# A copy-and-scale kernel that is limited by DMA: loads and stores moved into one queue in a fixed order

## The chip, the cores and the metric

The kernel runs on one core of one Trainium2 chip. The metric is the device time of one execution in microseconds (us), the median of several runs. A profile of one execution goes with it; its span is the time from the first to the last instruction on the core.

## The reference: what is computed

```python
def setup_inputs():
    batch, seq, hidden, n_experts = 16, 1024, 512, 8
    k = 2
    # x: [batch, seq, hidden] float32, expert_weights: [batch, seq, k] float32

def reference(x, expert_indices, expert_weights):
    x_expanded = x[:, :, np.newaxis, :].repeat(k, axis=2)
    weights = expert_weights[..., np.newaxis]
    return (x_expanded * weights).astype(np.float32)
```

Each of the 16,384 tokens has a row of 512 float32 numbers. The output holds two copies of each row, each multiplied by one weight. The indices are not used. So 33.55 MB of x go in and 67.11 MB go out, and there is one multiplication for each output element.

## The kernel before

Tokens are laid out with 128 consecutive ones in each partition (`A_TOTAL` = 128). One row of x in a partition has 2 KB, one row of the output (`row` = 1024 elements) 4 KB. The kernel takes 8 tiles of 16 tokens per partition. A tile of x is 32 KB in each partition, 4.19 MB in all; it is read in one transfer. The output is made in halves of 8 tokens, also 32 KB per partition, and each half is stored in one transfer.

```python
    xr = x.rearrange("b s h -> (b s) h").rearrange("(p a) h -> p (a h)", a=A_TOTAL)
    outr = out.rearrange("b s k h -> (b s) (k h)").rearrange(
        "(p a) n -> p (a n)", a=A_TOTAL)
    # ... (wr: the weights in the same layout)
    TX = 16
    TO = 8
    x_pool = ctx.enter_context(tc.tile_pool(name="x_pool", bufs=2))
    o_pool = ctx.enter_context(tc.tile_pool(name="o_pool", bufs=4))

    w_tile = w_pool.tile([P, A_TOTAL * k], f32)
    nc.sync.dma_start(out=w_tile, in_=wr)

    for i in range(A_TOTAL // TX):                      # 8 tiles
        x_tile = x_pool.tile([P, TX * hidden], f32)
        nc.scalar.dma_start(                            # loads: queue of ScalarE
            out=x_tile, in_=xr[:, i * TX * hidden : (i + 1) * TX * hidden])
        for j in range(TX // TO):                       # 2 halves
            o_tile = o_pool.tile([P, TO * row], f32)
            for t in range(TO):
                # ...
                for kk in range(k):
                    nc.vector.tensor_scalar(            # one row of 512, times one weight
                        out=o_tile[:, o : o + hidden],
                        in0=x_tile[:, at : at + hidden],
                        scalar1=w_tile[:, c : c + 1],
                        scalar2=None, op0=mybir.AluOpType.mult)
            first = (i * TX + j * TO) * row
            nc.sync.dma_start(                          # stores: queue of SyncE
                out=outr[:, first : first + TO * row], in_=o_tile)
```

Loads and stores are in two queues. A load can start as soon as one of the two x buffers is free, whatever the stores are doing. VectorE must wait when all four output buffers are still being stored.

Of the kernel before, what the change touches and what calls it, by code (L numbers as in the profile page):

```python
# [1 line left out]

# [4 lines left out]


@with_exitstack
def kernel(  # L10
    ctx: ExitStack,
    tc: tile.TileContext,
    x: bass.AP,
    expert_indices: bass.AP,
    expert_weights: bass.AP,
    out: bass.AP,
):
    nc = tc.nc

    batch, seq, hidden = x.shape  # L20
    k = expert_weights.shape[-1]
    P = nc.NUM_PARTITIONS
    ntok = batch * seq
    assert ntok % P == 0
    A_TOTAL = ntok // P

    xr = x.rearrange("b s h -> (b s) h").rearrange("(p a) h -> p (a h)", a=A_TOTAL)
    outr = out.rearrange("b s k h -> (b s) (k h)").rearrange(
        "(p a) n -> p (a n)", a=A_TOTAL
    )  # L30
    wr = expert_weights.rearrange("b s k -> (b s) k").rearrange(
        "(p a) k -> p (a k)", a=A_TOTAL
    )
    f32 = mybir.dt.float32
    row = k * hidden

    TX = 16
    TO = 8

    w_pool = ctx.enter_context(tc.tile_pool(name="w_pool", bufs=1))  # L40
    x_pool = ctx.enter_context(tc.tile_pool(name="x_pool", bufs=2))
    o_pool = ctx.enter_context(tc.tile_pool(name="o_pool", bufs=4))

    w_tile = w_pool.tile([P, A_TOTAL * k], f32)
    nc.sync.dma_start(out=w_tile, in_=wr)

    for i in range(A_TOTAL // TX):
        x_tile = x_pool.tile([P, TX * hidden], f32)
        nc.scalar.dma_start(
            out=x_tile, in_=xr[:, i * TX * hidden : (i + 1) * TX * hidden]  # L50
        )
        for j in range(TX // TO):
            o_tile = o_pool.tile([P, TO * row], f32)
            for t in range(TO):
                at = (j * TO + t) * hidden
                for kk in range(k):
                    c = (i * TX + j * TO + t) * k + kk
                    o = t * row + kk * hidden
                    nc.vector.tensor_scalar(  # L59
                        out=o_tile[:, o : o + hidden],  # L60
                        in0=x_tile[:, at : at + hidden],
                        scalar1=w_tile[:, c : c + 1],
                        scalar2=None,
                        op0=mybir.AluOpType.mult,
                    )
            first = (i * TX + j * TO) * row
            nc.sync.dma_start(out=outr[:, first : first + TO * row], in_=o_tile)


# [1 line left out]
_INS = ['x', 'expert_indices', 'expert_weights']  # L71
_OUTS = [((16, 1024, 2, 512), 'float32')]


# [23 lines left out]
```

## Time and profile before

| what | value |
|---|---|
| time, median of 3 runs | 241.06 us (240.87 to 241.54) |
| span of the profiled execution | 238.8 us |
| bytes moved by DMA | 100.81 MB: 33.69 MB read from HBM, 67.11 MB written |
| mean rate over the span | 422 GB/s |
| stores: 16 of 4.19 MB | median 44.9 us from issue to landing |
| loads of x: 8 of 4.19 MB | median 23.9 us from issue to landing |
| load of the weights: 1 of 0.13 MB | 10.1 us from issue to landing |
| one `tensor_scalar`, 128 x 512 float32 | 480 ns long; they overlap, 16 of them take 6.42 us |

The time from issue to landing includes the time in which a transfer stands behind others in its queue, or takes turns with those of the other queue. Queue q1 in the profile is that of SyncE (the weights and the stores), q10 that of ScalarE (the loads of x). A queue's share is the time that its packets took, as a share of the time of all 16 DMA engines over the span. A row of digits cuts the span into 40 slices, each digit giving the busy share in tenths. The DMA's packets have the size of one row in one partition: 32 KB for loads and stores, 1 KB for the weights, and 4 bytes for a completion signal.

### The profile page before, as it was taken

To read this page: it belongs to the slowest core of one execution; us is meant where nothing else is said; L and a number is where in the kernel's file an instruction comes from. 1 tells how busy PE (TensorE), PEld (TensorE's weight loads), DVE (VectorE), ACT (ScalarE), POOL (GpSimd) and SP (SyncE) were. 2 spreads that over 40 slices of the span, in tenths; PEclk is the share of its full clock that TensorE was granted. 3 is DMA by queue.
4 is the path that set the end of the run, shared out by engine and by line. 5 is a ranking of instruction groups with operands and counts; after the bars stand their busy time and mean duration, and the time that the engine had idled before them with its cause. 6 is when DMAs were issued, how large, how long until landed. Compare 5 with 4: busy or idle time off the path is not lost.

```text
span 238.8 us, 358 instructions
## 1 busy us (share of the span) xinstructions
DVE 102.5 (43%) x256; POOL 0.2 (0%) x4
## 2 busy tenths in 40 slices
DVE  0079994059701904682054910739008486400000
POOL 0000000000000000000000000000000000000000
DMA  7999999999999999999999999999999999999994
GB/s 277 447 439 417 434 380 417 439 439 439 423 423 428 439 423 412 439 439 439 439 439 434 434 439 439 412 435 428 428 423 434 434 439 439 439 439 434 434 439 214
DMA packets 3602, 100.81 MB, mean 422 GB/s; under 512 B 400, under 2 KB 528, under 8 KB 528
## 3 DMA queue, kind: packets, MB, share of 16 engines
q1 hardware_dynamic: 2448, 67.24, 65.4%
q10 hardware_dynamic: 1152, 33.55, 33.2%
q14 instruction: 2, 0.02, 0.0%
HBM read 33.69 MB, written 67.11 MB: 422 GB/s over the span
## 4 chain that ended last, share of the span: by engine, by line
DMA 62%; DVE 18%; another core or an unknown queue 5%; DVEq 0%; issue 0%
DMA out_dram<-o_tile 57%; DVE o_tile L59 18%; DMA x_tile<-in_x_dram 5%; DVEq L93 0%; DVEq L59 0%
## 5 line engine op out<-in xcount | busy, mean ns | idle before, releaser
L59 DVE TENSOR_SCALAR o_tile<-x_tile,w_tile 128x512 f32<-128x512 f32 x256 | 102.5, 480 | 103.3 <-DMA out_dram<-o_tile 74.1
L82 POOL MEMSET const-bfloat16-1.0<- 128x1 bf16 x1 | 0.1, 101 | 0.0
L82 POOL MEMSET const-uint8-127<- 128x1 uint8 x1 | 0.1, 101 | 0.0
L82 POOL MEMSET const-float32-0.0<- 128x1 f32 x1 | 0.1, 98 | 0.2 <-issue 0.2
L82 POOL MEMSET const-float32-1.0<- 128x1 f32 x1 | 0.1, 98 | 0.0
## 6 DMA issues: line engine op xcount, KB each, us to landing
out_dram<-o_tile SPq DMA_DIRECT2D x16, 4096.0 KB, 44.9
x_tile<-in_x_dram ACTq DMA_DIRECT2D x8, 4096.0 KB, 23.9
w_tile<-in_expert_weights_dram SPq DMA_DIRECT2D x1, 128.0 KB, 10.1
```

The lines of the kernel that those rows point to most:

```text
L59: nc.vector.tensor_scalar(out=o_tile[:, o : o + hidden], in0=x_tile[:, at : at + hidden], scalar1=w_tile[:, c : c + 1], scalar2=None, op0= ...
L82: nc = _bacc.Bacc("TRN2", target_bir_lowering=False, num_devices=1)
```

## The change

Loads and stores are all issued by SyncE into one queue, in an order that the program fixes. Of a pool of three slots of 64 KB per partition, each slot takes one tile: x is loaded into its upper half, VectorE writes the two scaled copies over the whole slot, and the slot is stored in one transfer of 64 KB per partition. The order of the tokens makes that safe: the outputs of token t take the place of x rows that have been used, and the last row is scaled in place. Loads stay at 32 KB per partition, but stores double in size, and there are 8 in place of 16. The weights move to the queue of ScalarE. The aim is that reads and writes of HBM come in long stretches in a fixed order and do not take turns packet by packet, and that fewer and larger transfers are made.

```diff
-    TX = 16
-    TO = 8
+    T = 16
+    SLOTS = 3
+    n_tiles = A_TOTAL // T
 ...
-    x_pool = ctx.enter_context(tc.tile_pool(name="x_pool", bufs=2))
-    o_pool = ctx.enter_context(tc.tile_pool(name="o_pool", bufs=4))
+    pool = ctx.enter_context(tc.tile_pool(name="slots", bufs=SLOTS))
 ...
-    nc.sync.dma_start(out=w_tile, in_=wr)
+    nc.scalar.dma_start(out=w_tile, in_=wr)
 ...                      (the loop of the kernel before is taken out)
+    x_at = T * (row - hidden)
+    slots = {}
+
+    def load(i):
+        slots[i] = pool.tile([P, T * row], f32, name="slot")
+        nc.sync.dma_start(
+            out=slots[i][:, x_at : x_at + T * hidden],
+            in_=xr[:, i * T * hidden : (i + 1) * T * hidden],
+        )
+
+    def scale(i):
+        slot = slots[i]
+        for t in range(T):
+            src = slot[:, x_at + t * hidden : x_at + (t + 1) * hidden]
+            for kk in range(k):
+                o = t * row + kk * hidden
+                c = (i * T + t) * k + kk
+                nc.vector.tensor_scalar(
+                    out=slot[:, o : o + hidden],
+                    in0=src,
+                    scalar1=w_tile[:, c : c + 1],
+                    scalar2=None,
+                    op0=mybir.AluOpType.mult,
+                )
+
+    def store(i):
+        nc.sync.dma_start(
+            out=outr[:, i * T * row : (i + 1) * T * row], in_=slots.pop(i)
+        )
+
+    for i in range(SLOTS):
+        load(i)
+    scale(0)
+    store(0)
+    for i in range(1, n_tiles):
+        scale(i)
+        store(i)
+        if i - 1 + SLOTS < n_tiles:
+            load(i - 1 + SLOTS)
```

In SyncE's queue this gives: load 0, load 1, load 2, store 0, store 1, load 3, store 2, load 4, store 3, load 5, store 4, load 6, store 5, load 7, store 6, store 7. Load 3 uses the slot of tile 0 and has to wait until store 0 has landed; load 4 waits for store 1, and so on.

More of the change, by code (lines that the diff above doesn't have):

```diff
@@ L35 @@
     row = k * hidden
-    TX = 16
-    TO = 8
+    T = 16
+    SLOTS = 3
+    n_tiles = A_TOTAL // T
     w_pool = ctx.enter_context(tc.tile_pool(name="w_pool", bufs=1))
-    x_pool = ctx.enter_context(tc.tile_pool(name="x_pool", bufs=2))
-    o_pool = ctx.enter_context(tc.tile_pool(name="o_pool", bufs=4))
+    pool = ctx.enter_context(tc.tile_pool(name="slots", bufs=SLOTS))
     w_tile = w_pool.tile([P, A_TOTAL * k], f32)
-    nc.sync.dma_start(out=w_tile, in_=wr)
[L47 to L50, printed above, removed]
-        )
[L52 to L67, printed above, removed]
```

## The prediction

> **What bounds the kernel now.** I read the page first: the busy time of the engines, the two DMA rows of the slices, the queue shares and the chain that ended last. Then I cut the span into stretches, and last looked at the single DMA packets.
>
> ```profile
> DVE 102.5 (43%) x256; POOL 0.2 (0%) x4
> DMA  7999999999999999999999999999999999999994
> q1 hardware_dynamic: 2448, 67.24, 65.4%
> q10 hardware_dynamic: 1152, 33.55, 33.2%
> DMA 62%; DVE 18%; another core or an unknown queue 5%; DVEq 0%; issue 0%
> L59 DVE TENSOR_SCALAR o_tile<-x_tile,w_tile 128x512 f32<-128x512 f32 x256 | 102.5, 480 | 103.3 <-DMA out_dram<-o_tile 74.1
> ```
>
> VectorE is busy 43% and spends as long waiting, mostly for a store to free an output buffer. That wait costs nothing by itself, because the DMA row stands at 9 in every slice but the first and the last: the stores are not late, they are queueing. The two data queues took 65.4 + 33.2 = 98.6% of the 16 engines' span. So only 1.4% of 238.8 us, 3.3 us, is idle DMA time. The chain's "DMA 62%" is not the measure here; a chain passes through VectorE while other transfers are running. The stretches show where the idle time and the slower spots lie (window, length, VectorE, GpSimd, clock, DMA share, GB/s):
>
> ```profile
> 0.00:20.00 20.00, 6.69 (x17) 0.20 (x4) 1.00 0.94 395
> 20.00:40.00 20.00, 18.74 (x48) 0.00 (x0) 1.00 1.00 405
> 40.00:57.00 17.00, 6.27 (x16) 0.00 (x0) 1.00 1.00 432
> 57.00:100.00 43.00, 19.43 (x49) 0.00 (x0) 1.00 1.00 433
> 100.00:180.00 80.00, 32.32 (x81) 0.00 (x0) 1.00 1.00 432
> 182.00:200.00 18.00, 11.30 (x29) 0.00 (x0) 1.00 1.00 430
> 200.00:236.00 36.00, 5.77 (x15) 0.00 (x0) 1.00 0.99 429
> ```
>
> From 40 to 180 us loads and stores share the engines, and they move 432 GB/s. After 182 us there are only stores (the last load lands at 181 us), in one queue, and they move 429 to 430. Mixed and unmixed traffic run at one speed. The packet records say the same: 2899 of the 3072 data packets (32 KB each, one per partition row) took exactly 1213 ns on their engine, loads and stores alike, so 16 x 32768 B / 1.213 us = 432 GB/s. All 3072 at that pace take 3072 x 1.213 / 16 = 232.9 us. The span is 238.8, so **everything this change could win lies in 5.9 us**, which divide so:
> - about 2.0 us before the first data packet and 1.1 us after the last one;
> - 0.5 us for the weights: 128 packets of 1 KB at 65 ns, over 16 engines; and 0.2 us for 400 semaphore packets of 9 ns;
> - 1.7 us of data packets longer than 1213 ns, nearly all of them loads. They come in bursts: the first packets of the first load (0.28 us per engine), the loads in flight when the first stores set in at 20.8 us (0.36 us), and again at 30 to 37 us (0.8 us). This is the 405 GB/s of the second stretch. Later load starts cost almost nothing (0.2 us for five of them).
>
> The remainder, some 0.4 us, is rounding and engines that end a little apart.
>
> **What the Trainium skill says.** "DMA: Bandwidth & Descriptors", section "Where 436 GB/s comes from", puts the ceiling at 435.2 GB/s for the 16 ports. The 432 of the trace agrees, and leaves 0.7% at most. The same page, "Issuing engines are not separate DMA queues", says that transfers issued from several engines run on the same 16 DMA engines and interleave; the trace agrees, one load and one store in flight together have the bandwidth of one. "Queues, rings and completion order" says that descriptors of one ring are consumed in order, and that an engine takes turns between the queues it has work for, packet by packet. The weights bear that out: 8 packets per engine taking turns with 8 packets of x should need 8 x 1.3 us, and the load of w lands after 10.1 us. So one queue replaces turns by a fixed order, not by more bandwidth. "SBUF — State Buffer", section on the SBUF size, gives about 208 KiB usable per partition. Three slots of 64 KB and 1 KB of weights fit, a fourth slot does not; no run shows that here.
>
> **The change part by part.**
> Bytes: unchanged, 33.55 MB of x in, 67.11 MB out. At 432 GB/s a load of 4.19 MB takes 9.7 us, a store of 8.39 MB 19.4 us. 232.9 us stay.
> Issues: 16 stores of 332 ns become 8, from the same SyncE; they were never on the path. Saved: eight times 16 semaphore packets of 9 ns, below 0.1 us.
> Packet size: if the 64 KB row of a store goes as one packet, one fixed cost in two is saved. An estimate from the page's 435.2 GB/s: 32768 B need 1204.7 ns, the trace has 1213, so 8.3 ns are fixed; 1024 x 8.3 ns / 16 = 0.5 us saved. If the row is split into 32 KB packets, nothing.
> VectorE: the same 256 instructions at 0.40 us pitch (16 in 6.42 us), so 12.8 us a tile. Scaling in place adds waits of VectorE on itself from token 8 on, when outputs are written over inputs; most wait for instructions finished long ago. I allow up to 2 us a tile, 13 to 15 us.
> Order: what must be shown is that the single ring never runs dry. Data begin at 2.0; x of tile 0 lands at 13.3 as now, so store 0 is issued at about 27, while loads 1 and 2 keep the ring busy to 32. Stores 0 and 1 fill it to 71. Load 3 waits for store 0 (landed at 52) and is issued 19 us before its turn. From there the ring reads load 3, store 2, load 4, store 3 and so on. A tile lands, and store and load of the ring (29 us) run while VectorE needs 15: a slack of some 14 us. The tightest place is the last one: load 7 lands at about 197, store 6 covers 19.4 us, and scaling (15), landing and starting a store (0.4 + 1.3) need 16.7. **Slack 2.7 us, so no gap.** VectorE then stays hidden everywhere, as now.
> Read starts: a load behind a store in the same ring may expose the latency of its first packets. The two clean cases of now are 0.28 and 0.36 us; five such loads give 0 to 1.6 us, in place of the 1.4 us that the bursts after 20 us cost today.
> Sum: 232.9 + 0.5 (w) + 0.2 + 0.3 (first load) + 0 to 1.6 - 0 to 0.5 + 3.1 (both ends) = 236.5 to 238.6 us of span. The remainder that I couldn't place (0.4) put on top, the middle is 237.9, against 238.8 now: **0.9 us less**, and 241.06 - 0.9 = 240.2 us.
>
> **The rivals.**
> 1. Order pays: reads and writes in separate phases run faster than mixed ones, and the gain is several per cent. For it speaks only the dip to 405 GB/s at 20 to 40 us, worth 20 x 27/432 = 1.3 us. Against it, 432 mixed and 430 stores alone. With all dips and the packet cost gone the span would be some 236.4, and the time about 238.7, still only 1%.
> 2. The ring turns around badly: each change between store and load (some 12) lets the engine drain. With 0.4 us each it is 5 us more, about 245. Against it, today engines change direction at nearly every packet without losing anything; but there the two directions sit in different queues, so the trace has no case of a load directly behind a store in one ring.
> 3. The ring runs dry, because a load stands behind a store that waits for VectorE. If the scaling took 18 us, not 13 to 15, only the last tile would show it, with 1 to 2 us. A later first store doesn't matter before 32 us.
> 4. One 64 KB packet is slower than two of 32 KB. Nothing in the profile shows such a packet, so I can't exclude it; 1% more on each is 1.6 us.
>
> **Range and chances.** The median time stands 2.3 us above the profiled span (241.06 and 238.8). A gain above 2% needs a time below 236.2, that is a span near 234, which is 232.9 us of packets plus 1.1 us for both ends: practically excluded. A loss above 2% needs 4.8 us, so rival 2 at its full size, or two rivals together. I take 238.7 to 242.6 as the range, more room above than below, since all that can go wrong adds.
>
> **What would show it.** In the profile after: the DMA shares of the queues again add up to 98% or more; the slices at 9 throughout; 430 to 434 GB/s in any stretch of the middle; store landings 19.4 us apart and loads 9.7 us when both queue; VectorE waiting for loads instead of stores, about 100 us busy. Slices that drop at every change of direction would show rival 2; a gap at about 216 us, before the last store, rival 3. A rate above 435 would show that my ceiling is wrong, and the prediction with it.

## The result, and the profile after

The changed kernel takes 250.64 us (250.4 to 250.87), the kernel before beside it 241.08. The ratio is **1.0388, with a 95% interval of 1.0362 to 1.0413: slower**. The prediction was 240.2 us, with a range to 242.6. It was wrong.

The page of the changed kernel, the same parts as shown of before: engines, DMA by slices, queues, and the group of scalings.

```profile
span 248.8 us, 333 instructions
DVE 103.3 (42%) x256; POOL 0.2 (0%) x4
DMA  7999999899899999999999999999989999999992
q1 hardware_dynamic: 2304, 100.66, 97.9%
q10 hardware_dynamic: 144, 0.13, 0.2%
L66 DVE TENSOR_SCALAR slot<-slot,w_tile 128x512 f32<-128x512 f32 x256 | 103.3, 479 | 119.2 <-DMA slot<-in_x_dram 105.1
```

The DMA engines are as busy as before, 98.1% of a longer span, and they move the same bytes. So nothing ran dry: the packets themselves took longer. Stretches of the changed kernel (window, length, VectorE, GpSimd, clock, DMA share, GB/s):

```profile
5.00:28.00 23.00, 14.36 (x36) 0.00 (x0) 1.00 0.99 428
64.00:72.00 8.00, 0.00 (x0) 0.00 (x0) 1.00 1.02 393
98.00:118.00 20.00, 1.51 (x4) 0.00 (x0) 1.00 1.01 383
128.00:150.00 22.00, 3.81 (x10) 0.00 (x0) 1.00 1.01 399
213.00:240.00 27.00, 9.45 (x24) 0.00 (x0) 1.00 0.99 430
```

Only loads (5 to 28 us) and only stores (213 to 240 us) run at 428 and 430 GB/s. Wherever the queue goes from a store to a load and back, as at 64 to 72, 98 to 118 and 128 to 150 us, it is 383 to 399 with the engines still busy. (A packet counts in the stretch in which it starts, so the rate of a short stretch is to be read with its share: 393 GB/s at a share of 1.02 are 385 for busy engines.) The DMA records show it packet by packet. An undisturbed 32 KB packet takes 1213 ns, an undisturbed 64 KB packet 2418 ns. The first loads behind a store, the last two loads ahead of a store and the last store packet ahead of a load take mostly 0.1 to 1.2 us more, the longest 1.4. I call the sum of what goes beyond the undisturbed time, divided by 16 engines, the **stretched time**: 10.9 us after, 1.7 before. A second sum is the idle DMA time in the last 12 us of transfers, because the engines end apart: 2.2 us after, 1.0 before. So +9.3 and +1.2, less 0.5 for half as many store packets, make 10.0 us, and that is the difference of the spans (248.8 and 238.8).

### The profile page after: what moved, and what is told of

The parts are those of the page before. It is cut to its first block, busy times and chain, and to the rows that moved or that the text cites. A ratio compares the mean times of both kernels' runs of the same rounds, so it can differ in the third digit from the quotient of the medians.

```text
span 248.8 us, 333 instructions
## 1 busy us (share of the span) xinstructions
DVE 103.3 (42%) x256; POOL 0.2 (0%) x4
## 4 chain that ended last, share of the span: by engine, by line
DMA 68%; DVE 21%; issue 0%; DVEq 0%; SPq 0%
DMA slot<-in_x_dram 34%; DMA out_dram<-slot 29%; DVE slot L66 21%; DMA w_tile<-in_expert_weights_dram 5%; DVEq L66 0%; SPq L54 0%
## 5 line engine op out<-in xcount | busy, mean ns | idle before, releaser
L66 DVE TENSOR_SCALAR slot<-slot,w_tile 128x512 f32<-128x512 f32 x256 | 103.3, 479 | 119.2 <-DMA slot<-in_x_dram 105.1
```

Of the source, the lines that this page charges most:

```text
L66: nc.vector.tensor_scalar(out=slot[:, o : o + hidden], in0=src, scalar1=w_tile[:, c : c + 1], scalar2=None, op0=mybir.AluOpType.mult,)
```

## The experiments

Each was compared with the kernel before on the same chip (its median there was 242.6 to 243.5 us), so ratios are compared. All compute the whole reference. The two sums at the right are each from one profiled execution. That of before is of an execution of 240.5 us in the first comparison, so the row of before serves as a mark, and the other rows are best compared with each other.

| run | queues | packets, load / store | ratio to before (95%) | stretched us | ends apart us |
|---|---|---|---|---|---|
| before | 2 | 32 / 32 KB | 1 | 1.7 | 1.0 |
| after | 1 | 32 / 64 | 1.0388 (1.0362 to 1.0413) | 10.9 | 2.2 |
| e1 | 2 | 32 / 64 | 1.0251 (1.0197 to 1.0305) | 6.5 | 0.1 |
| e2 | 1 | 32 / 32 | 1.0150 (1.0109 to 1.0192) | 6.1 | 2.8 |
| e3 | 1, 21 changes | 16 / 32 | 1.0260 (1.0202 to 1.0319) | 8.7 | 2.2 |
| e4 | 1, 5 changes | 16 / 32 | 1.0043 (1.0025 to 1.0061) | 4.1 | 1.1 |
| e5 | 2 | 32 / 32 | 0.9954 (0.9931 to 0.9976) | 2.7 | 1.7 |
| e6 | 2 | 32 / 64 | 1.0260 (1.0201 to 1.0319) | 3.1 | 2.0 |
| e7 | 1 | 32 / 16 | 1.0105 (1.0070 to 1.0140) | 4.1 | 3.2 |
| e8 | 1 | 16 / 16 | 1.0085 (1.0061 to 1.0110) | 3.0 | 3.5 |
| e9 | 1, engines staggered | 32 / 32 | 1.0355 (1.0318 to 1.0392) | 6.9 | 3.6 |
| e10 | 1, engines staggered | 32 / 64 | 1.0444 (1.0413 to 1.0475) | 10.7 | 2.2 |
| e11 | 2 | 16 / 32 | 1.0247 (1.0204 to 1.0290) | 2.7 | 6.4 |
| e12 | 1, engines staggered | 32 / 32 | 1.0161 (1.0107 to 1.0215) | 3.7 | 2.7 |

A "change" is a place where the queue goes from load to store or back; the changed kernel, e2, e7 and e8 have 11.

**e1: loads in a queue of their own.**

```diff
     def load(i):
-        nc.sync.dma_start(
+        nc.scalar.dma_start(
```

> The changed kernel with its loads issued by ScalarE into ScalarE's queue (behind the weights); slots, sizes and waits stay. Theory (a change of direction inside one queue costs about 1 us: the changed kernel has 11 of them and 11 us of stretched packets): with the loads in a queue of their own nothing changes direction inside a queue, 239 to 241 us, load packets mostly 1213 ns, 64 KB store packets 2418 ns. Rival A (the 64 KB packets are slower): stays at 249 to 251. Rival B (scaling in place in a shared slot, or three slots only, holds up the transfers): stays at 248 to 251.

It stayed at 1.025, so my theory fell in this form: one queue alone is not the cause. But the loss has another shape here. Two stretches of e1 and the last scaling of its timeline:

```profile
55.00:205.00 150.00, 51.76 (x128) 0.00 (x0) 1.00 1.01 423
215.00:230.00 15.00, 11.01 (x28) 0.00 (x0) 1.00 0.71 306
213.07 13.01 DVE L66 TENSOR_SCALAR slot<-slot,w_tile 128x512 f32<-128x512 f32 x32 [18.21 <-DMA slot<-in_x_dram]
```

The two queues take turns by packet, and with 64 KB against 32 KB the loads get a third of the engines. Load 7 is issued at 174.5 us and lands only after 38.4 us; the last store can't be issued before 226, and the engines stand idle for some 5 us (DMA share 0.71). The share of the engines is only part of that delay: load 7 is signed off by its first engine after 27.5 us, and by its last 11 us later, so far had the engines drifted apart. Stretched time is 6.5, of which 1.3 falls at 25 to 35 us, when stores set in behind the first loads.

**e2: stores cut into two transfers of 32 KB per partition**, still one queue and one order.

```diff
-            out=outr[:, i * T * row : (i + 1) * T * row], in_=slots.pop(i)
+ ...                       (slot = slots.pop(i), half = T * row // 2)
+        for h in range(2):
+            nc.sync.dma_start(
+                out=outr[:, (2 * i + h) * half : (2 * i + h + 1) * half],
+                in_=slot[:, h * half : (h + 1) * half],
+            )
```

> The changed kernel with each store cut into two transfers of 32 KB per partition, issued one behind the other into the same queue. Theory (change of direction): the number of changes stays at 11, so 250 to 252 us, with the stretched packets still next to the changes. Rival A (64 KB packets): 239 to 241, as all packets are 32 KB again.

Neither: 1.015, in between. Stretches of e2:

```profile
28.00:40.00 12.00, 11.93 (x31) 0.00 (x0) 1.00 1.01 394
66.00:88.00 22.00, 3.24 (x9) 0.00 (x0) 1.00 1.00 395
88.00:100.00 12.00, 9.70 (x25) 0.00 (x0) 1.00 1.01 437
100.00:118.00 18.00, 1.59 (x5) 0.00 (x0) 1.00 1.00 391
138.00:235.00 97.00, 38.82 (x96) 0.00 (x0) 1.00 1.00 430
```

The early changes (28 to 40, 66 to 88 and 100 to 118 us) run at 391 to 395 GB/s, but the last two loads and their four changes, all after 138 us, cost 0.5 us of stretched time together: 430. The landings of the 16 engines give a hint why. Each transfer is signed off by every engine: within 0.8 us up to 63 us, within 1.6 at 85, 3.0 at 116, and 3.9 to 4.2 from 146 us on. **The engines drift apart, and as they do, the changes become free.**

**e3 and e4: the number of changes.** Halved tiles, six slots; e3 keeps the order, e4 groups it.

```diff
-    T = 16
-    SLOTS = 3
+    T = 8
+    SLOTS = 6
 e4 besides: the loop is now
+    for g in range(0, n_tiles, SLOTS):
+        group = range(g, min(g + SLOTS, n_tiles))
+        for i in group: load(i)
+        for i in group: scale(i); store(i)
```

> Tiles of half the size (8 tokens, stores 32 KB, loads 16 KB per partition), six slots, the same order: after the first loads one load behind each store. The changes of direction rise from 11 to 21, the bytes stay. Theory (about 1 us for each change): 239.5 + 21 = 259 to 262 us. Rival C (a load's packets are slow in proportion to their bytes when they stand in one queue with stores): stays at 249 to 252. Rival A: 240 to 241.

> The same halved tiles and six slots in one queue, but in groups: six loads, six stores, six loads, six stores, four loads, four stores. 5 changes of direction. Theory (about 1 us for each change): 239.5 + 5 = 244 to 246 us. Rival C (by bytes): 249 to 252. Rival A: 240 to 241.

e4 came close to its number; e3 was far below it (its 21 changes cost 8.1 of the 8.7 us, not 21), and again its changes after 125 us were almost free, at a spread of the landings of 3.2 to 3.8 us. In e4, where the spread stays at 0.7 to 1.9 us, each change can be seen alone:

```profile
36.00:84.00 48.00, 12.17 (x31) 0.00 (x0) 1.00 1.01 435
84.00:96.00 12.00, 0.00 (x0) 0.00 (x0) 1.00 0.97 380
96.00:116.00 20.00, 17.86 (x45) 0.00 (x0) 1.00 1.00 430
124.00:174.00 50.00, 13.36 (x33) 0.00 (x0) 1.00 1.00 432
174.00:200.00 26.00, 13.14 (x33) 0.00 (x0) 1.00 1.00 411
```

Between changes 430 to 435, at the changes of 84 to 96 and 174 to 200 us 380 and 411. Its five changes cost 0.8, 1.0, 0.35, 0.7 and 0.5 us of stretched time. So a fixed cost per change fails, and so does a cost by bytes.

**e5: both taken away**, loads in their own queue and stores cut to 32 KB (the edits of e1 and e2).

> Loads in a queue of their own as in e1, and each store cut into two transfers of 32 KB per partition as in e2; slots and scaling in place stay. What the first four runs left: the single queue alone is not the cause (e1), the 64 KB packet is part of it (e2), and changes of direction inside one queue stretch the packets beside them (e4: nothing stretched but at its 5 changes). New theory: two things add, the packet size of the stores and the changes inside one queue. Then with both taken away 239.5 to 242 us, on a level with the kernel before, stretched time below 2.5 us. Rival (slots and waits cost by themselves): 244 or more.

0.9954: with both parts undone the slots and the scaling in place cost nothing, and this is the version that beats both kernels, if by half a per cent. Its stretched time of 2.7 us is just above the 2.5 that I had allowed. Its stretches:

```profile
20.00:40.00 20.00, 19.52 (x49) 0.00 (x0) 1.00 1.00 407
55.00:195.00 140.00, 53.40 (x132) 0.00 (x0) 1.00 1.00 430
195.00:236.00 41.00, 12.94 (x32) 0.00 (x0) 1.00 1.00 432
```

It runs as the kernel before did, with the same dip when the stores set in.

**e6: the kernel before with 64 KB output buffers.**

```diff
-    TO = 8                      # and o_pool bufs=4
+    TO = 16                     # and o_pool bufs=2
```

> The kernel before, with only its output buffers doubled to 64 KB (two of them), so that a store has 64 KB per partition; two queues, x buffers of its own. New theory: the 64 KB packets stretch loads that take turns with them, 4 to 6 us in all as in e1, so 244 to 249 us, some of it perhaps as a dry ring. Rival (64 KB is bad only in one queue with its changes): 240 to 241.

The time of 249.7 us is a little above the expected range, and not for the expected reason: its stretched time is only 3.1 us.

```profile
20.00:34.00 14.00, 14.00 (x37) 0.00 (x0) 1.00 0.67 242
34.00:230.00 196.00, 82.02 (x206) 0.00 (x0) 1.00 1.00 430
```

With two x buffers and whole tiles to be scaled before a store, more than 5 us of DMA time are idle at the start (share 0.67), where neither load 2 nor store 0 is issued before the first tile is scaled, at 26.8 us. So 64 KB in two queues costs here mainly by that wait. The 64 KB packets are shown to stretch others next to changes (after against e2) and in e1 (6.5 us, e5 2.7), not in general. Why e1 and e6 differ in this is open.

**e7 and e8: packets of 16 KB**, stores in four transfers, in e8 loads in two as well.

> The changed kernel, one queue and 11 changes, each store cut into four transfers of 16 KB per partition; loads stay at 32 KB. Theory that a change costs by the store packet beside it: 64 KB gave 10.9 us of stretched time, 32 KB 6.1, so 16 KB should give 3 to 4.5 and 243.5 to 246 us. Rival (16 engines that drift apart no longer change at once, which is why the later changes of e2 and e3 were free): no more than 1 us away from e2.

> As e7, and the loads also cut into two transfers of 16 KB per partition. Theory (packet size on both sides of a change): 2 to 3.5 us of stretched time, below e7 by about 1 us. Rival (only the store packets matter): the same as e7 plus 0.5 us for the larger number of packets.

Both ways a step down, to 4.1 and 3.0 us of stretched time, but the ratios fall by only 0.5 and 0.2 points, and their intervals overlap. The gain goes mostly into the packets themselves: two of 16 KB take 1222 ns where one of 32 KB takes 1213, which is 1.2 us in e7 and 0.6 more in e8; and the engines end 0.3 and 0.4 us further apart.

Stores of 64, 32 and 16 KB give 10.9, 6.1 and 4.1 us of stretched time. Most of the difference comes late. The first three changes (15 to 92 us) cost 3.2, 2.9 and 2.3 us, the eight later ones 7.3, 2.5 and 1.2. So while the engines are close together a change costs nearly the same beside 64 KB packets as beside 32 KB; what the large packets do is to keep the later changes dear. With them the engines also drift apart more slowly (2.3 us at 147 us, in e2 3.9).

**e9, e10, e12: the engines staggered from the start.** To test whether it matters that all engines change together, three small loads go ahead of everything, work for some engines only. What they write is overwritten later.

```diff
+ ...                       (slots[0] is made here; stores are cut as in e2)
+    for lo, hi in ((0, 8), (8, 12), (12, 14)):
+        nc.sync.dma_start(
+            out=slots[0][lo:hi, : T * hidden], in_=xr[lo:hi, : T * hidden])
     for i in range(SLOTS):
         load(i)
```

> e2 (one queue, stores cut to 32 KB packets) with three small loads put in front of everything, of 8, 4 and 2 rows of 32 KB, into a part of the first slot that is written over later. They are extra work for some of the 16 DMA engines only (up to three packets, 3.6 us, if 8 rows go to 8 engines, and so on), so that the engines reach each change of direction apart. In e2 a change cost 1.2 us and more while all engines landed within 0.8 us of each other, and nearly nothing once they had drifted 4 us apart. Theory (a change costs because all engines change together): the spread of the first landings is 3 to 4 us, the stretched time falls from 6.1 to 1.5 to 3.5 us, and the first change at 30 us costs less than 0.5. The time itself hardly moves (244 to 247), as the extra packets delay the last engine by as much. Rival (the early changes are dear for another reason, such as addresses or tile number): stretched time 5.5 to 6.5 us as in e2, and a time of 248 to 251.

The time and the stretched time are worse than expected, the main point is clear. Stretches of e9: the start, the first five changes (they lie later here, and each window is as long as that of e2 or longer), and the end:

```profile
5.00:15.00 10.00, 0.00 (x0) 0.00 (x0) 1.00 0.96 213
35.00:47.00 12.00, 11.93 (x31) 0.00 (x0) 1.00 1.01 432
73.00:95.00 22.00, 1.92 (x5) 0.00 (x0) 1.00 1.01 427
104.00:124.00 20.00, 3.87 (x10) 0.00 (x0) 1.00 1.02 441
138.00:235.00 97.00, 38.81 (x96) 0.00 (x0) 1.00 1.00 432
```

The changes that ran at 394, 395 and 391 GB/s in e2 now run at 432, 427 and 441. After the first 15 us, all 11 changes together cost 0.8 us of stretched time, in e2 5.4; the landings are 5.4 us apart. What made it slow is the start: at 5 to 15 us only 213 GB/s, with packets of 2 to 4 us, 6.1 us lost.

> The same three small loads in front of the changed kernel itself, with its 64 KB stores. Its engines drifted to 4 us apart as well, but its late changes still cost up to 0.9 us. Theory: a spread has to be large against a packet, and 3.6 us is only one and a half packets of 64 KB; so the stretched time falls little, from 10.9 to 8 to 10 us, and the time is 250 to 254. If it falls to 4 or less, the packet size counts only through the spread.

The total of 10.7 hides the same split: 6.3 us in the first 15 us, 4.4 after it, where the changed kernel had 10.4. So staggering takes away more than half of the cost with 64 KB packets too, with the landings 4.2 to 5.9 us apart, and not all.

In e12 the rows of the small loads are spread (every fourth partition: `slots[0][lo:hi:4]`, `xr[lo:hi:4]`, from partitions 0, 64 and 80).

> e9 with the rows of the three small loads spread out (every fourth partition, in different blocks) instead of neighbouring rows. In e9 nothing was stretched at the changes any more, but the first 15 us ran at half speed, 6.1 us lost, so that the time rose. If that loss came from neighbouring partitions being written by several DMA engines at once, it goes here: the first 15 us at over 400 GB/s, stretched time of the whole 1 to 2 us, and a time 1.000 to 1.008 of the kernel before (e2: 1.015). If the first loads are slow because the engines start apart, whatever the rows, it stays at 1.03 and over.

```profile
5.00:15.00 10.00, 0.00 (x0) 0.00 (x0) 1.00 0.92 347
28.00:40.00 12.00, 11.93 (x31) 0.00 (x0) 1.00 1.00 429
66.00:88.00 22.00, 0.45 (x2) 0.00 (x0) 1.00 0.99 413
100.00:118.00 18.00, 1.07 (x4) 0.00 (x0) 1.00 1.01 431
```

The expectation was met in part. The start loses 2.2 us in place of 6.1, at 347 GB/s and not over 400. The 11 changes cost 1.6 us; at 66 to 88 us, where the landings were 2.3 to 2.7 us apart, 0.8 us remained. But the ratio of 1.016 is that of e2. What the changes no longer cost is spent at the start: against e2, 1.5 us more of stretched time, 1.5 us more of idle engines, and 1.1 us for the extra rows; the ends are as far apart as there (2.7 and 2.8 us). Staggering is a test here, not a remedy.

**e11: meant as the best version**, e3 with its loads in the queue of ScalarE, so that taking turns gives loads a third of the bytes.

> A version meant to be the best: two queues as before, slots with scaling in place as in the change, tiles of 8 tokens: loads 16 KB and stores 32 KB per partition, six slots. Taking turns by packet then gives loads one third of the bytes, which is their share of the whole, so that no load is late or early. Theory: as e5 or a little better, ratio to before 0.992 to 0.997; stretched time 1.5 to 2.5 us. Rival (the smaller packets cost what is won: 2048 packets of 16 KB at 611 against half of 1213 ns are 0.6 us): 0.997 to 1.002.

A miss. Up to 230 us it is as quick as any (stretched time 2.7), then 13 of the 16 engines sign off the last store by 238.2 us, and the last one at 244.7:

```profile
230.00:245.50 15.50, 0.00 (x0) 0.00 (x0) 1.00 0.46 199
```

Why that engine fell behind, in a spread of landings that grew to 8.7 us, was not settled.

## Why the prediction was wrong, step by step

**What held.** The bound was read rightly: DMA engines at 98%, the same before and after. The undisturbed 64 KB packet takes 2418 ns, 8 ns less than two of 1213; that agrees with the fixed part I had estimated as 8.3 ns from the 435.2 GB/s in the Trainium skill, "DMA: Bandwidth & Descriptors", section "Where 436 GB/s comes from". VectorE needs 13.0 us a tile in place, within the 13 to 15 allowed. The ring never ran dry, as rival 3 would have had it. The last tile, from the timeline of the changed kernel:

```profile
191.98 30.90 SPq L75 DMA_DIRECT2D out_dram<-slot  x2
209.51 13.01 DVE L66 TENSOR_SCALAR slot<-slot,w_tile 128x512 f32<-128x512 f32 x32 [17.57 <-DMA slot<-in_x_dram]
```

The scaling ends at 222.5, the last store is issued then, and store 6 is signed off by its first engine at 224.7 and by its last at 228.7.

**What failed** is the term "Read starts": five loads at 0 to 0.3 us, 1.6 us at most. Measured, all changes together cost 10.4 us (10.9 less 0.5 at the first load). Two errors made it small. I counted only loads behind stores, while the last loads ahead of a store are stretched too: the six changes from load to store make 4.9 of the 10.4 us. So it was 11 changes and not 5. And I took 0.28 and 0.36 us as the clean cases and set aside the 0.8 us of the burst at 30 to 37 us, as something of the start. It is nearer to what the runs show: 0.35 to 1.0 us for each change in e4, and 0.95 on average in the changed kernel. The sum also had nothing for engines that drift apart, which cost another 1.2 us at the end.

**Rival 2** ("the ring turns around badly", 0.4 us each, about 245) had the right place and half the size, but its sign, slices that drop at each change, did not show: the engines stay busy (98.1%), with longer packets. I set it against the kernel before, whose engines change direction at nearly every packet for nothing. That was the wrong inference. For stores of 32 KB, e2, e3, e9 and e12 show that a change is dear when all 16 engines make it together: the first one costs 1.1 us in e2, at a spread of the landings of 0.8 us; the last four cost 0.5 us together at 4 us, and all 11 cost 0.8 us at 5.4 (e9). In one queue the engines come to a change together as long as they have not drifted apart. In two queues loads and stores alternate on each engine all the time; that this is why e5 loses so little is likely, but no run shows it by itself. Rival 1, the aim of the change, had it the wrong way round: long stretches of one direction run no faster (428 to 435) than mixed traffic (432), and only add the changes.

**Rival 4** (64 KB packets) was judged by the packet alone, which is innocent. Beside a change it is not: cutting the stores to 32 KB takes the ratio from 1.039 to 1.015 and the stretched time from 10.9 to 6.1. The two parts roughly add up: with neither 0.995, with one queue 1.015, with 64 KB stores 1.025 (e1, where part of the loss is the wait for the last load), with both 1.039.

What happens in the chip at such a change is open. The records show packets that take longer, not what they wait for. Also open is why larger packets keep the later changes dear (4.4 us in e10 at landings 4.2 to 5.9 us apart, 0.8 in e9 at 5.4). That a spread of 4 us is less than two 64 KB packets may be part of it; it is not shown.

## What to carry to other kernels

Where DMA engines are already busy 98% of the span and mixed traffic runs as fast as one direction alone, an order of transfers has nothing to win: add up the packets first. A single queue that goes back and forth between loads and stores pays at each change as long as the engines are in step; use two queues that take turns (e5), or few and long groups (e4). And choose packet sizes for the turns they take, since a queue with packets twice as large gets twice the share, and a late load can leave the last store waiting.

## What the runs showed of the hardware

- A change of direction in one queue costs 0.35 to 1.0 us of every engine's time while the engines land 0.7 to 1.9 us apart (e4), and 0.8 us for 11 changes when they are 5.4 us apart (e9); both with stores of 32 KB.
- Engines drift apart. In one queue they do so at the changes: in e2 the landings are 0.8 us apart in all transfers from 34 to 63 us, 1.6 at 85 and 4.2 at the end. But changes in one queue are not the only way: with two queues and store packets twice the size of the loads', e1 came to 11.0 us and e11 to 8.7. The end pays for it, with 1.1 to 3.6 us of idle DMA time in the runs with one queue and 6.4 in e11, against 1.0 in the kernel before; only e1, where the engines stood waiting before the last store, ended together (0.1).
- Small loads for a few engines were slow: 32 KB packets took 2 to 4 us for rows in neighbouring partitions at the start of e9. The Trainium skill, "SBUF — State Buffer", section "Door 1: The DMA port swizzle", says that four neighbouring partitions share a DMA port, and spreading the rows (e12) took the loss from 6.1 to 2.2 us, which agrees. But in e9 the first packets of the large loads on all engines were as slow, which that does not explain.
